# A hybrid SSM and attention layer with experts: scan outputs and turns of k later, queries by block, one norm of o in the output projection

## The chip, the core and the metric

One NeuronCore of a Trainium2 chip runs the whole layer in one launch. The metric is device time in microseconds (us), from one execution of the program. The core's engines run side by side: PE (TensorE, matmuls and transposes), DVE (VectorE) and ACT (ScalarE) and POOL (GpSimd) for element-wise work, SP for issuing DMAs. They meet through semaphores; each engine executes its own instructions in the order in which the program gives them.

## What is computed

One layer, one sequence of 1024 tokens, width 1024, fp32:

```python
mod = silu(c) @ ada_w + ada_b            # sh1, sc1, g1, sh2, sc2, g2
h = rms_norm(x, norm1_g) * (1 + sc1) + sh1
u, q, k, v, f, hc, bg, cg = split(h @ w_in)
y_ssm  = s5(u)              # 16 groups of 16 channels, 64 complex states: scan, gelu, gated unit
y_attn = fox_attention(q, k, v, f)   # 8 heads of 64, causal, q and k normed,
                                     # logits + cum(log f)_q - cum(log f)_k
y_conv = bg * conv3(cg * hc)
y = rms_norm(concat(y_ssm, y_attn, y_conv), per head of 64) * out_norm_g
x = x + g1 * (y @ w_out)
h = rms_norm(x, norm2_g) * (1 + sc2) + sh2
x = x + g2 * moe(h)         # 16 experts in 4 groups, best group, top 2, SwiGLU of width 512
```

## The kernel before, in words

Every fp32 product is made of three matmuls on parts: an operand is split into a high part (ACT, a copy to the matmul's type) and a low part (DVE, the rest); high by high, low by high and high by low are added in PSUM (L293, L295, L298). So each operand costs ACT one pass, DVE one pass and PE three.

The stages, with their time in the profiled execution: modulation and norm of x (to about 55 us); the convolution's projections (to 120); the u projection with the preparation of the scan (`s5_prep`, to 153); q projection, 16 tiles, with the scan (`s5_main`, to 245); k projection, 16 tiles, with the rest of the modulation (`ada2`, to 341); attention (to 534); the w_out stage, 8 tiles of 128 tokens (to 650); routing (to 690); the experts (to the end).

The order is written by hand. Side work is written as generators: `step` advances the scan's by a given number of yields after each projection tile, so the number of plain yields in a generator says beside which tile a piece of it stands. Four such numbers matter here.

- In `s5_prep` two plain yields stand ahead of the four groups pg (L716 and L718 on PE, copied to gk by ACT at L720). Beside them on PE, `conv_norm` puts small matmuls pn (L950) between the matmuls of a u tile; they read zt, which ACT squares at L942 in four pieces.
- `PY` plain yields stand in `s5_main` between the scan's last elementwise steps (vv on DVE) and the four groups py (L855, L856, L858: 4 times 3 matmuls each), which ACT takes through the gelu (L860). Then come eight turns pt (L876, L877) and the gated unit.
- A q or k tile's result (pm, two PSUM buffers) is copied to r by ACT (L1162) with its squares (L1167). After four tiles `qk_norm` puts four steps into a list by the number of tiles by which each is later: norm, split (ks, buffered once), and two turns (L1090 on PE, evicted by ACT or DVE at L1098). `QC, QD` are these distances for q, `KC, KD_` for k.
- In attention, a unit is one head and two blocks of 128 queries with all keys up to them: score (L1298, L1299 with the low part, L1300 the mask), shift by the decay with the running minimum (DVE, L1316), exponential (ACT, L1327), transposes of the logits (L1340), their split into ph (ACT, L1345) and pl (DVE, L95), the product with v (L1360, L1361), and the gather of o (L1374). There are 32 units, four lots m of eight heads; two heads' groups hg of 4 share one load of q, whose parts are kept in DRAM (`qtd`). `load_q` brings both blocks of a group into one tile of 2048 columns; the ring holds one such tile in the first half of the stage and two after head unit 12, where pools are exchanged. At its end the weight rows of w_out are split too (woh on ACT, wol on POOL).

The output norm of attention's o is made per lot of two token blocks by `norm_o(m)`: squares and sums (on POOL for m below `NP`, otherwise ACT and DVE), then an inverse square root in small DVE steps of 128x16 (L1407, L1408, L110 to L115), then the multiplication into o_all. Lots 0, 1 and 2 are made inside attention, lot 3 in the w_out stage, at tiles i = 2 to 4.

The w_out stage, per tile of 128 tokens: `w_prep` transposes the scan's rows (ysm) and o and splits them to yh and yl; `w_mm` makes two halves of 512 columns in PSUM (pmw, two buffers); `w_x1` applies gate and residue on DVE, which frees pmw; `w_h2` makes the second norm, with POOL adding a row and storing. `steps` advances the norm of o between them.

Expert weights are loaded by SP as their buffers come free.

Of the kernel before, what the change touches and what calls it, by code (L numbers as in the profile page):

```python
# [8 lines left out]
F32 = mybir.dt.float32  # L9
# [35 lines left out]
EB = 1  # L45
NP = 3
WS = 48
WT = 4
PB = 4
QC, QD, KC, KD_ = 3, 6, 2, 4  # L50
EA = (1, 0, 0, 2)
# [4 lines left out]
XB = 1  # L56
PY = 5
UG = 6
# [23 lines left out]
def _emit(tc, nc, V, A, G, T, I, out, dump, upto, stack):  # L82
# [11 lines left out]
    def tt(o, a, b, op, eng=None):  # L94
        (eng or V).tensor_tensor(o, a, b, op=op)  # L95
# [547 lines left out]
    def s5_prep():  # L643
# [53 lines left out]
        for n in range(2):  # L697
# [6 lines left out]
            yield  # L704
        yield
        yield

# [511 lines left out]
    with ExitStack() as esa:  # L1219
        pa1 = esa.enter_context(tc.tile_pool(name="pa1", bufs=2, side="right"))  # L1220
        lgr, phr, plr_, qtr = Ring("lg", S), Ring("ph", 512), Ring("pl", 512), Ring("qt", 2048)
        lgr.add(pa1, 3)
        phr.add(pa1, 2)
        plr_.add(pa1, 2)
        qtr.add(pa1, 1)
        ost = pa1.tile([P, 16, HD], F32, name="ost", bufs=1)
# [30 lines left out]

        def load_q(g):

            qt = qtr.tile(F32R)[:].rearrange("p (b n c) -> p b n c", b=2, n=2)  # L1260
            m, hg = g // 2, g % 2
            for b in range(2):
                src = qtd[2 * m + b, hg]
                nc.sync.dma_start(out=qt[:, b, 0, :].bitcast(F32), in_=src)
                nc.sync.dma_start(out=qt[0:64, b, 1, :].bitcast(F32), in_=src[64:P, :])
                nc.sync.dma_start(out=qt[64:P, b, 1, :].bitcast(F32), in_=src[0:64, :])
            qts[m, hg] = qt

# [15 lines left out]
        def score(u, b):  # L1284

            if u >= len(units):
                return
            m, h = units[u]
            w = P * (2 * m + b + 1)
            if (u, b) == (16, 0):  # L1290
                es_s.close()
                ps_s.append(es_s.enter_context(tc.tile_pool(name="ps_s2", bufs=2, space=PSUM)))
            sp = ps_s[-1].tile([P, 512 if m < 2 else S], F32, name="sp", tag="s")
            qt = qts[m, h // 4]
            qs = [qt[:, b, n, (h % 4) * P:(h % 4) * P + P] for n in range(2)]
            for n0 in range(0, w, 512):
                n1 = min(n0 + 512, w)
                T.matmul(sp[:, n0:n1], lhsT=qs[0], rhs=kT[:, h, n0:n1], start=True, stop=False)  # L1298
                T.matmul(sp[:, n0:n1], lhsT=qs[1], rhs=kT[:, h, n0:n1], start=False, stop=n1 != w)  # L1299
            T.matmul(sp[:, w - P:w], lhsT=identB, rhs=maskB, start=False, stop=True)  # L1300
            sps[u, b] = sp
# [83 lines left out]
        def norm_o(m, pool, sq):  # L1385
# [26 lines left out]
            rs = got[0]  # L1412
            tt(ov, ov, rs[:, :, None].to_broadcast([P, 16, HD]), ALU.mult, G if m < 3 else V)

# [20 lines left out]
        def v_end():  # L1435
            while v_done:
                v_out(*v_done.pop(0))

        load_q(0)
        for u in range(2):  # L1440
# [23 lines left out]
        for n, (u, kp) in enumerate(steps):  # L1464
# [14 lines left out]
            for b in bs:  # L1479
                shift(u + 2, b)  # L1480
            v_end()
            if 1 in bs:
                if not second and 4 * len(qts) == u + 3:
                    load_q(len(qts))
                if u == 12:
                    es_v.close()
                    es_w.close()
                    es_h.close()
                    op_ = es_o.enter_context(tc.tile_pool(name="op_", bufs=1, side="left"))
                    o_all = op_.tile([P, NT, NH, HD], F32, name="o_all")  # L1490
                    wo = es_wo.enter_context(tc.tile_pool(name="wo", bufs=1, side="left"))
                    pa = esa.enter_context(tc.tile_pool(name="pa", bufs=2, side="left"))
                    lgr.add(pa, 3)
                    phr.add(pa, PB - 2)
                    plr_.add(pa, PB - 2)
                    qtr.add(pa, 1)
                    for g in saved:
                        nc.gpsimd.dma_start(out=o_all[:, g // 2 * 2:g // 2 * 2 + 2, g % 2 * 4:g % 2 * 4 + 4, :],
                                            in_=od[g].rearrange("p (b h d) -> p b h d", b=2, h=4))
                    norms.append(norm_o(0, pa, ost))  # L1500
                    second = True
                if second and 4 * len(qts) <= u + 4 < len(units):
                    load_q(len(qts))
                load_n(u + 4)
# [8 lines left out]
            if second and len(wait) >= (LW if n > 18 else 1):  # L1513
                finish()
            if h == 1 and kp == m and m > 1:
                norms.append(norm_o(m - 1, pa, ost))
# [216 lines left out]
    with ExitStack() as esw:  # L1733
# [16 lines left out]
        def w_prep(i, ld):  # L1750
# [5 lines left out]
            of = o_all[:, i].rearrange("p h d -> p (h d)")  # L1756
            for k0, n in ((0, 2), (2, 4)):
                pt = ps_y.tile([P, 512], F32, name="pty", tag="y")
# [96 lines left out]
        for i in range(NT):  # L1855
            x1 = x1s[i] = pw.tile([P, D], F32, name="x1", tag="x1")
            pm = w_mm(y, 0)
            if i == 1:
# [4 lines left out]
                V.tensor_copy(c0, pl)  # L1863
            if i == 2:
                last_o = norm_o(3, pw, pw.tile([P, 16, HD], F32, name="sqo", tag="sq", bufs=1))
            if 2 <= i < 5:
                steps(last_o, 2)
            ny = w_prep(i + 1, ld.get(i + 1))
# [431 lines left out]
```

## Time and profile before

| | |
|---|---|
| median of 3 runs (lowest, highest) | 1094.33 us (1094.05, 1100.98) |
| the profiled execution | 1096.41 us, span 1094.7 us |
| PE busy | 1010.8 us, 92% of the span |
| DVE, ACT, POOL busy | 735.6, 520.8, 244.2 us |
| PE's mean granted clock, share of full speed | 0.957 |

The profile is one execution on the hardware. A slice is a fortieth of the span, 27.4 us; busy shares of an engine come in tenths. PEclk is the clock granted to PE, as a share of full speed. In the timeline a row is an instruction or several alike in a row: start, length, engine, line of the kernel, operation, out<-in, shape and, in brackets, the idle time of the engine just before it with what ended it.

### The profile page before, as it was taken

The numbers are of one execution on the slowest core, as the hardware profiler recorded it, in microseconds if no ns is written. First come the engines' busy times: TensorE is split into PE (matmuls) and PEld (weight loads), VectorE is DVE, ScalarE is ACT, GpSimd is POOL, SyncE is SP. The second block draws the span as 40 slices with busy tenths as digits, with TensorE's granted clock in tenths as the row PEclk, the third lists the DMA queues.
The fourth block names the chain that finished last, engine by engine and source line by source line (L and its number), as shares of the span: only waits on it lengthen the run. The fifth ranks groups of instructions, "written<-read, shape, count | busy, mean of one in ns | idle before, by whom it ended". The sixth has DMA issues, their size and how long they took to land. (4 is left out here: it accounts for less than half of the span.)

```text
span 1094.7 us, 17976 instructions
## 1 busy us (share of the span) xinstructions
PE 1010.8 (92%) x6273; PEld 823.8 (75%) x6273; DVE 735.6 (67%) x1608; ACT 520.8 (48%) x1102; POOL 244.2 (22%) x275
## 2 busy tenths in 40 slices
PE   4999999799999998998899994999999999999995
PEld 2767779788778977987788883777777777777774
DVE  5779525826544344787566778896556999789593
ACT  3531214235444555776522223655344676567470
POOL 2019001001110002237222134212333312122121
PEclk9999899879999998998899995999999999999998
DMA  9801145106784444554436625896778899969782
GB/s 316 265 14 46 30 103 104 49 20 228 262 296 147 115 127 120 168 182 147 138 121 212 226 106 188 288 353 230 237 229 285 264 375 358 375 233 356 257 268 42
DMA packets 105472, 215.61 MB, mean 197 GB/s; under 512 B 16658, under 2 KB 39680, under 8 KB 105216
## 3 DMA queue, kind: packets, MB, share of 16 engines
q1 hardware_dynamic: 92368, 171.19, 46.6%
q0 software_dynamic: 12000, 40.37, 13.3%
q10 hardware_dynamic: 992, 2.63, 0.6%
q8 instruction: 61, 1.00, 0.4%
q14 instruction: 51, 0.42, 0.1%
HBM read 185.47 MB, written 28.10 MB: 195 GB/s over the span
## 5 line engine op out<-in xcount | busy, mean ns | idle before, releaser
L95 DVE TENSOR_TENSOR wel<-wer,weh 128x1024 fp32r<-128x1024 f32 x192 | 223.2, 1217 | 2.2 <-DVEq L2170 1.3
L1953 ACT ACTIVATE weh<-wer 128x1024 fp32r<-128x1024 f32 x192 | 189.0, 1053 | 5.1 <-DVE oh L1962 1.7
L2008 POOL DMA_INDIRECT out_dram<-y,idx x28 | 64.2, 2293 | 221.1 <-DVE y L2073 136.3
L2036 PE MATMUL pg<-weh,xh 128*128 128x512 f32 x256 | 104.8, 409 | 2.0 <-ACT hid L2194 0.7
L2037 PE MATMUL pg<-weh,xl 128*128 128x512 f32 x256 | 103.1, 403 | 0.0
L95 DVE TENSOR_TENSOR pl<-ptp,ph 128x512 fp32r<-128x512 f32 (+1 forms) x80 | 50.2, 635 | 38.9 <-ACT ph L1345 38.7
L2041 PE MATMUL pg<-wel,xh 128*128 128x512 f32 x256 | 66.3, 397 | 0.0
L2036 PEld LDWEIGHTS pg<-weh,xh 128*128 128x128 f32 x256 | 49.1, 192 | 17.9 <-issue 6.1
L1345 ACT ACTIVATE ph<-ptp 128x512 fp32r<-128x512 f32 (+1 forms) x80 | 44.1, 553 | 29.7 <-PE ptp L1340 29.4
L2037 PEld LDWEIGHTS pg<-weh,xl 128*128 128x128 f32 x256 | 49.2, 192 | 11.5 <-DVE xl L95 0.4
L2041 PEld LDWEIGHTS pg<-wel,xh 128*128 128x128 f32 x256 | 47.7, 188 | 11.2
L1327 ACT ACTIVATE lg<-lg,mn 128x128 f32<-128x128 f32 (+3 forms) x64 | 49.5, 773 | 11.0 <-DVE mn L1316 11.0
L2063 PE MATMUL pd<-weh,hh 128*128 128x512 f32 x128 | 52.3, 409 | 0.7 <-ACT hh L2055 0.5
L1340 PE MATMUL ptp<-identF,lg 128*128 128x128 f32 x288 | 47.7, 283 | 5.5 <-DVE pl L95 5.3
L293 PE MATMUL pmw<-woh,yh 128*128 128x512 f32 x128 | 52.7, 412 | 0.0
L295 PE MATMUL pmw<-woh,yl 128*128 128x512 f32 x128 | 51.1, 400 | 0.0
L2064 PE MATMUL pd<-wel,hh 128*128 128x512 f32 x128 | 50.6, 395 | 0.0
L2022 ACT ACTIVATE xh<-ptx 128x512 fp32r<-128x512 f32 x32 | 19.2, 599 | 61.8 <-issue 58.6
L1360 PE MATMUL po<-ph,vs 128*128 128x256 f32 (+1 forms) x160 | 47.1, 315 | 1.1 <-ACT ot L1364 1.0
L1162 ACT ACTIVATE r<-pm 128x256 f32<-128x256 f32 x32 | 12.4, 386 | 73.3 <-PE pm L298 54.6
L1992 POOL DMA_INDIRECT xg<-h2d,idx x16 | 22.1, 1380 | 89.2 <-DVE wgt L1979 85.8
L1361 PE MATMUL po<-pl,vs 128*128 128x256 f32 (+1 forms) x160 | 40.2, 285 | 0.1
(660 smaller groups left out, 2635.1 us busy)
## 6 DMA issues: line engine op xcount, KB each, us to landing
wer<-in_w_up_dram SPq DMA_DIRECT2D x64, 512.0 KB
wer<-in_w_gate_dram SPq DMA_DIRECT2D x63, 512.0 KB
wer<-in_w_down_dram SPq DMA_DIRECT2D x63, 512.0 KB
adw<-in_ada_w_dram SPq DMA_DIRECT2D x32, 512.0 KB
vroom<-in_ada_w_dram SPq DMA_DIRECT2D x16, 512.0 KB
xt<-in_x_dram SPq DMA_DIRECT2D x14, 512.0 KB
qtd<-qe POOLq DMA_DIRECT2D x16, 256.0 KB, 7.8
qt<-qtd SPq DMA_DIRECT2D x16, 256.0 KB
```

The lines of the kernel that those rows point to most:

```text
L95: (eng or V).tensor_tensor(o, a, b, op=op)
L293: T.matmul(o, lhsT=sh(k), rhs=mh(k), start=(k == 0), stop=False)
L295: T.matmul(o, lhsT=sl(k), rhs=mh(k), start=False, stop=False)
L1327: A.activation(lg[:, :w], lg[:, :w], AF.Exp, bias=mn, scale=-1.0, accum_out=l_all[:, qb, h:h + 1])
L1340: T.transpose(pt[:, c0:c0 + P], lgs[u, b][0][:, k0:k0 + P], identF)
L1953: A.activation(hi, raw, AF.Copy)
L2008: G.indirect_dma_start(out=out[:, :], out_offset=bass.IndirectOffsetOnAxis(ap=ix, axis=0), in_=y, in_offset=None, compute_op=ALU.add)
L2036: T.matmul(pg, lhsT=x[0][:, k, :], rhs=hi, start=(k == 0), stop=False)
L2037: T.matmul(pg, lhsT=x[1][:, k, :], rhs=hi, start=False, stop=False)
L2041: T.matmul(pg, lhsT=x[0][:, k, :], rhs=lo, start=False, stop=(k == KD - 1))
L2063: T.matmul(pd, lhsT=h[0][:, k, :], rhs=hi[:, n, :], start=(k == 0), stop=False)
L2064: T.matmul(pd, lhsT=h[0][:, k, :], rhs=lo[:, n, :], start=False, stop=False)
```

## The change

Seven numbers or places: four plain yields instead of two in `s5_prep`; `PY` 8 instead of 5; `KD_` 5 instead of 4; `load_q` loads one block of queries into a tile of 1024 columns, in a ring of twice as many tiles; `NP` 2 instead of 3, with which lot 2 of `norm_o` goes to the w_out stage, three steps at tiles 0 and 1 each; and in the first `w_prep` the transposes of o stand ahead of those of ysm.

```diff
-NP = 3
+NP = 2
-QC, QD, KC, KD_ = 3, 6, 2, 4
+QC, QD, KC, KD_ = 3, 6, 2, 5
-PY = 5
+PY = 8
...
-        yield
-        yield
+        for _ in range(4):
+            yield
...
-qtr.add(pa1, 1)
+qtr.add(pa1, 2)
...
-        def load_q(g):
-
-            qt = qtr.tile(F32R)[:].rearrange("p (b n c) -> p b n c", b=2, n=2)
-            m, hg = g // 2, g % 2
-            for b in range(2):
-                src = qtd[2 * m + b, hg]
-                nc.sync.dma_start(out=qt[:, b, 0, :].bitcast(F32), in_=src)
-                nc.sync.dma_start(out=qt[0:64, b, 1, :].bitcast(F32), in_=src[64:P, :])
-                nc.sync.dma_start(out=qt[64:P, b, 1, :].bitcast(F32), in_=src[0:64, :])
-            qts[m, hg] = qt
+        q_at = [0, 0]
+
+        def load_q(b):
+
+            qt = qtr.tile(F32R)[:].rearrange("p (n c) -> p n c", n=2)
+            m, hg = q_at[b] // 2, q_at[b] % 2
+            q_at[b] += 1
+            src = qtd[2 * m + b, hg]
+            nc.sync.dma_start(out=qt[:, 0, :].bitcast(F32), in_=src)
+            nc.sync.dma_start(out=qt[0:64, 1, :].bitcast(F32), in_=src[64:P, :])
+            nc.sync.dma_start(out=qt[64:P, 1, :].bitcast(F32), in_=src[0:64, :])
+            qts[m, hg, b] = qt
...
-            tt(ov, ov, rs[:, :, None].to_broadcast([P, 16, HD]), ALU.mult, G if m < 3 else V)
+            tt(ov, ov, rs[:, :, None].to_broadcast([P, 16, HD]), ALU.mult, G if m < 2 else V)
...
+            for b in bs:
+                if not second and 4 * q_at[b] == u + 3:
+                    load_q(b)
...
-                if second and 4 * len(qts) <= u + 4 < len(units):
-                    load_q(len(qts))
+                for b in range(2):
+                    if second and 4 * q_at[b] <= u + 4 < len(units):
+                        load_q(b)
...
-            if h == 1 and kp == m and m > 1:
+            if h == 1 and kp == m == 2:
...
-            for k0, n in ((0, 2), (2, 4)):
+            for k0, n in ((0, 2), (2, 4)) if i else ((2, 4), (0, 2)):
...
-            if i == 2:
-                last_o = norm_o(3, pw, pw.tile([P, 16, HD], F32, name="sqo", tag="sq", bufs=1))
-            if 2 <= i < 5:
-                steps(last_o, 2)
+            if i in (0, 2):
+                last_o = norm_o(2 + i // 2, pw, pw.tile([P, 16, HD], F32, name="sqo", tag="sq", bufs=1))
+            if i < 5:
+                steps(last_o, 3 if i < 2 else 2)
```

How it moves the instructions, at three places. In the first, ACT in the q projection, r is the copy of a projection tile's result, sq its squares, and the row with py is the gelu of one or two py groups. Before:

```order
L1098 ACTIVATE qe<-ptk 128x512
L1076 ACTIVATE ks<-r_1618 128x16x64
L1162 ACTIVATE r_2063<-pm 128x256
L1167 ACTIVATE sq,ss<-pm 128x64 x4
L280 ACTIVATE wh__1907<-wr__1767 128x2x256
L860 ACT_TABLE_LOAD
L860 ACTIVATE vroom<-py 128x4x8x16 x2
L1162 ACTIVATE r_2063<-pm 128x256
L1167 ACTIVATE sq,ss<-pm 128x64 x4
L860 ACTIVATE vroom<-py 128x4x8x16 x2
```

And of the change:

```order
L1162 ACTIVATE r_2063<-pm 128x256
L1167 ACTIVATE sq,ss<-pm 128x64 x4
L280 ACTIVATE wh__1907<-wr__1767 128x2x256
L1162 ACTIVATE r_2063<-pm 128x256
L1167 ACTIVATE sq,ss<-pm 128x64 x4
L860 ACT_TABLE_LOAD
L860 ACTIVATE vroom<-py 128x4x8x16
L1162 ACTIVATE r_2063<-pm 128x256
L1167 ACTIVATE sq,ss<-pm 128x64 x4
L1098 ACTIVATE qe<-ptk 128x512
L280 ACTIVATE wh__1907<-wr__1911 128x2x256
L860 ACTIVATE vroom<-py 128x4x8x16 x2
```

The first py group now follows two projection tiles instead of one and comes alone; the second and third stand a tile further on, and the fourth behind one more. PE has the same order of tiles and groups.

In the second place, DVE late in attention, pl is the low part of transposed logits, lg and mn the shift, and l, ro_i, ro_y and ro_t are the small steps of the norm of lot 2. Before:

```order
L95 TENSOR_TENSOR pl<-ptp,ph 128x512
L95 TENSOR_TENSOR pl<-ptp,ph 128x384
L1407 SCALAR_TENSOR_TENSOR l_5611<-f_sb 128x16
L1408 SCALAR_TENSOR_TENSOR l_5611<-sso,l_5611 128x16
L95 TENSOR_TENSOR pl<-ptp,ph 128x512
L1316 ISA lg,mn<-sp,nqb 128x896
L1316 ISA mn 128x1
L110 TENSOR_SCALAR ro_i<-l_5611 128x16
L111 TENSOR_SCALAR ro_y<-ro_i 128x16
L113 SCALAR_TENSOR_TENSOR ro_t<-ro_y 128x16
L114 TENSOR_TENSOR ro_t<-ro_t,l_5611 128x16
L115 SCALAR_TENSOR_TENSOR ro_y<-ro_t,ro_y 128x16
```

And of the change, where the line of the shift has become L1318:

```order
L95 TENSOR_TENSOR pl<-ptp,ph 128x512
L95 TENSOR_TENSOR pl<-ptp,ph 128x384
L95 TENSOR_TENSOR pl<-ptp,ph 128x512
L1318 ISA lg,mn<-sp,nqb 128x896
L1318 ISA mn 128x1
```

The small steps are gone from here, and the splits stand as before.

In the third place, DVE at the first tile of the w_out stage, s2r, bs and wrs are rows and weights of the second norm and the router, yl the low part of the next tile, and x the product that frees pmw. Before:

```order
L1836 SCALAR_TENSOR_TENSOR s2r<-s2r,n2r 128x1024
L1842 SCALAR_TENSOR_TENSOR bs_6045<-bs_6045,pv 128x8
L95 TENSOR_TENSOR wrs<-wr,bs_6045 128x128
L95 TENSOR_TENSOR yl<-pty,yh 128x256
L95 TENSOR_TENSOR yl<-pty,yh 128x512
L95 TENSOR_TENSOR yl<-cvt,yh 128x256
L95 TENSOR_TENSOR x_6071<-pmw,g1r 128x512
```

And of the change:

```order
L95 TENSOR_TENSOR wrs<-wr,bs_6027 128x128
L1406 TENSOR_REDUCE sso<-sqo 128x16
L1409 SCALAR_TENSOR_TENSOR l_6083<-f_sb 128x16
L1410 SCALAR_TENSOR_TENSOR l_6083<-sso,l_6083 128x16
L110 TENSOR_SCALAR ro_i<-l_6083 128x16
L111 TENSOR_SCALAR ro_y<-ro_i 128x16
L113 SCALAR_TENSOR_TENSOR ro_t<-ro_y 128x16
L114 TENSOR_TENSOR ro_t<-ro_t,l_6083 128x16
L115 SCALAR_TENSOR_TENSOR ro_y<-ro_t,ro_y 128x16
L95 TENSOR_TENSOR yl<-pty,yh 128x256
L95 TENSOR_TENSOR yl<-pty,yh 128x512
L95 TENSOR_TENSOR yl<-cvt,yh 128x256
```

A reduce and seven small steps now stand between wrs and the first yl; x follows behind the yl as before.

## Rows read from the trace of the kernel before

**Rows 1.** Page, part 2: busy tenths of PE and DMA in 40 slices
```profile
PE   4999999799999998998899994999999999999995
...
DMA  9801145106784444554436625896778899969782
```

**Rows 2.** Windows: stretch, us, busy PE, PEld, DVE, ACT, POOL (instructions); PEclk, DMA share, GB/s
```profile
120.77:152.69 31.92, 29.71 (x145) 22.55 (x144) 7.38 (x21) 6.69 (x12) 0.00 (x0) 0.79 0.23 47
...
206.28:226.55 20.27, 14.77 (x51) 11.03 (x49) 14.29 (x25) 3.60 (x12) 1.63 (x3) 0.62 0.20 65
226.55:231.70 5.15, 5.15 (x25) 5.15 (x25) 0.00 (x0) 0.60 (x1) 0.00 (x0) 0.51 0.00 0
231.70:240.12 8.42, 8.42 (x51) 6.48 (x49) 0.00 (x0) 1.80 (x10) 0.00 (x0) 1.00 0.01 2
```

**Rows 3.** Timeline of PE and ACT, u projection (start, us, instruction, idle before)
```profile
122.54 0.39 PE L718 MATMUL pg<-can,vroom 64*16 64x128 f32 x2 [1.38 <-DVE can L693]
...
125.49 0.38 PE L950 MATMUL pn<-blkF,zt 128*128 128x2 f32 x2 [0.81 <-ACT zt L942]
...
121.37 0.64 ACT L280 ACTIVATE wh__1211<-wr__1011 128x528 fp32r<-128x528 f32 x1
...
124.82 2.17 ACT L942 ACTIVATE zt<-hcs 128x512 f32<-128x512 f32 x4
```

**Rows 4.** Timeline of PE and ACT, first py groups
```profile
209.00 0.49 PE L856 MATMUL py<-car,vv 64*128 64x128 f32 x2 [2.34 <-DVE vv L95]
212.65 0.79 PE L858 MATMUL py<-can,vv 64*128 64x128 f32 x2 [3.16 <-DVE vv L95]
...
218.76 0.39 ACT L1162 ACTIVATE r<-pm 128x256 f32<-128x256 f32 x1 [13.21 <-DVE rk_m L123]
```

**Rows 5.** Timeline of PE, k projection
```profile
297.21 0.54 PE L1090 MATMUL ptk<-identR,ks 128*128 128x128 f32 x4 [2.12 <-ACT qe L1098]
```

**Rows 6.** Waits: engine, line, waited for: us in total, times, longest
```profile
PE sp L1299 <- DMA qt<-qtd: 4.5, 5, 1.9
```

**Rows 7.** Timeline of PE, POOL and DVE, late in attention
```profile
495.65 0.55 PE L1374 MATMUL oT<-ii,ot 128*128 128x64 f32 x4
502.11 0.56 PE L1374 MATMUL oT<-ii,ot 128*128 128x64 f32 x4
510.29 0.55 PE L1340 MATMUL ptp<-identF,lg 128*128 128x128 f32 x3 [2.87 <-DVE pl L95]
511.15 0.63 PE L1374 MATMUL oT<-ii,ot 128*128 128x64 f32 x4
521.22 0.56 PE L1374 MATMUL oT<-ii,ot 128*128 128x64 f32 x4
...
506.84 2.34 POOL L95 TENSOR_TENSOR wol<-wor,woh 128x1024 fp32r<-128x1024 f32 x1
...
506.94 2.28 DVE L113 SCALAR_TENSOR_TENSOR ro_t<-ro_y 128x16 f32<-128x16 f32 x1
509.46 0.17 DVE L115 SCALAR_TENSOR_TENSOR ro_y<-ro_t,ro_y 128x16 f32<-128x16 f32 x1
```

**Rows 8.** Windows: the low clock in attention's last units (columns as in rows 2)
```profile
511.75:518.45 6.70, 5.94 (x22) 4.85 (x21) 4.05 (x10) 4.88 (x8) 4.28 (x2) 0.51 0.04 13
```

**Rows 9.** Timeline of PE and DVE, w_out stage
```profile
536.53 0.66 PE L1761 MATMUL pty<-identF,ysm 128*128 128x128 f32 x2 [2.64 <-DMA cvt<-cd]
552.07 0.39 PE L293 MATMUL pmw<-woh,yh 128*128 128x512 f32 x1
...
550.33 0.68 DVE L95 TENSOR_TENSOR x<-pmw,g1r 128x512 f32<-128x512 f32 x1
565.58 0.69 DVE L95 TENSOR_TENSOR x<-pmw,g1r 128x512 f32<-128x512 f32 x1 [2.50 <-PE pmw L298]
571.44 1.21 DVE L1404 TENSOR_REDUCE sso<-sqo 128x16 f32<-128x1024 f32 x1
585.91 2.35 DVE L111 TENSOR_SCALAR ro_y<-ro_i 128x16 int32<-128x16 int32 x1
```

More of the change, by code (lines that the diff above doesn't have):

```diff
@@ L1220, in _emit @@
         pa1 = esa.enter_context(tc.tile_pool(name="pa1", bufs=2, side="right"))
-        lgr, phr, plr_, qtr = Ring("lg", S), Ring("ph", 512), Ring("pl", 512), Ring("qt", 2048)
+        lgr, phr, plr_, qtr = Ring("lg", S), Ring("ph", 512), Ring("pl", 512), Ring("qt", 1024)
         lgr.add(pa1, 3)
@@ L1293, in score @@
             sp = ps_s[-1].tile([P, 512 if m < 2 else S], F32, name="sp", tag="s")
-            qt = qts[m, h // 4]
-            qs = [qt[:, b, n, (h % 4) * P:(h % 4) * P + P] for n in range(2)]
+            qt = qts[m, h // 4, b]
+            qs = [qt[:, n, (h % 4) * P:(h % 4) * P + P] for n in range(2)]
             for n0 in range(0, w, 512):
@@ L1437, in v_end @@
                 v_out(*v_done.pop(0))
-        load_q(0)
+        for b in range(2):
+            load_q(b)
         for u in range(2):
@@ L1481, in _emit @@
             v_end()
+            for b in bs:
+                if not second and 4 * q_at[b] == u + 3:
+                    load_q(b)
             if 1 in bs:
-                if not second and 4 * len(qts) == u + 3:
-                    load_q(len(qts))
                 if u == 12:
@@ L1495, in _emit @@
                     plr_.add(pa, PB - 2)
-                    qtr.add(pa, 1)
+                    qtr.add(pa, 2)
                     for g in saved:
@@ L1501, in _emit @@
                     second = True
-                if second and 4 * len(qts) <= u + 4 < len(units):
-                    load_q(len(qts))
+                for b in range(2):
+                    if second and 4 * q_at[b] <= u + 4 < len(units):
+                        load_q(b)
                 load_n(u + 4)
```

## The prediction

> **What bounds the kernel now.** I read the page's slices first: TensorE (PE) is nearly full in all but the first slices, and in the long second half, the experts, it stands at 8 and 9 while the DMA engines stand at 7 to 9, not full throughout [rows 1]. So a microsecond that PE saves ahead of the experts should come out at the end, as long as the expert weights, loaded as buffers come free, move forward with it. The question is then where PE waits and where its granted clock is low ahead of the experts. The waits of PE by what ended them, and the timeline around each, lead to five places that the diff touches: the u projection, the first py groups in the q projection, the turns of k, the last head units of attention, and the first tiles of the w_out stage. Windows over these give the clock. In the rows the reader is to look at the bracket (idle before, and who ended it) and at PEclk: 1.00 is 2.4 GHz, about 0.5 is 1.2 GHz.
>
> **The change part by part.** The profiled execution took 1096.41 us (span 1094.7, the rest lies around it); the median of the runs shown is 1094.33. All terms below are differences, and I apply the sum to the median.
>
> *1. pg two steps later.* PE waits 1.38 us at the first pg group for can, which VectorE (DVE) has just begun, and 0.81 us at the first pn for the square zt on ScalarE (ACT) [rows 3]. The second wait is made by the first: gk, which needs pg, stands ahead of the four squares on ACT, so they start at 124.82 though ACT's split ended at 122.01 [rows 3]. After, the squares follow that split directly; the first is done some 0.6 us later (2.17 for four), and pn, which PE now reaches right after 120.77 and one matmul, waits about 1.6 us in one piece. Idle: 2.19 less 1.6, -0.6. The u projection's 31.92 us ran at a mean clock of 0.79 with PE busy 29.71 [rows 2]: with a lower level of half the speed, 0.21 of this is 6.7 us at stake. The idle piece comes earlier, but it is not smaller than each of the two before, so I expect most of the low clock again and count a fifth of the 6.7 back: -1.4. **-2.0** (from -5, the clock mostly held, to +1, the second pg group that now stands later among the pn pairs costing a third low piece).
>
> *2. py three steps later.* Before, PE reaches py at 206.28, two tiles ahead of its data, waits 2.34 us for the first half of vv and 3.16 for the second, and both py groups then run mostly at the lower level: 20.27 us for 24 matmuls with PEclk 0.62, against 8.42 for the next two py groups at 1.00 [rows 2, 4]. The project tile behind them still runs at 0.51, in 5.15 us [rows 2]; half of that, 2.6, at full speed. Lost before: 20.27 - 8.42 + 2.55 = 14.4 us, of which 5.5 are idle. After (the order rows), one more project tile stands ahead of py0 and fills 206.3 to about 209.1. The data of vv are made by DVE, whose chain the change does not touch, so its second half still comes at 212.65 [rows 4] and py0 waits about 2.7 of it. Then a new wait: the tile after py0 needs a PSUM buffer of pm, of which there are two, and both are held by tiles that ACT empties only from 218.76 on, when DVE's q norm lets it [rows 4]. With py0 done at 216.0 to 216.5, PE idles about 3 us more. Idle after: 5.7, no less than before. What is gained is the low stretch: py1 is no longer behind the gap, so one py group and one tile (3.2 + 2.6, the first being half of 14.77 - 8.42) can be low instead of two groups and a tile; I take 4.4 for it, some of this having come back by then. 14.4 - 5.7 - 4.4 = **-4.3** (from -8.7, no low clock at all, to 0, as long a low stretch as before).
>
> *3. Turns of k one tile later.* The ptk transposes wait once for ACT's qe buffer, 2.12 us [rows 5]; a project tile later ACT has had about 3 us more. The tile that comes ahead needs nothing from them. **-1.5** (-2.1, the wait, to +1, the last turns falling into the v tiles).
>
> *4. q by block.* Scores wait five times for the load of qt, 4.5 us in all, longest 1.9 [rows 6]. The ring holds the same bytes before and after; what a block gains is that its half comes free after its own score, one unit step sooner, and that the first score does not wait for the second half's three transfers. The two longest waits stand where the pools are changed at head unit 12 and the ring is refilled; there the transfers come in the same order as before. So only the other waits shrink: **-1.0** (-3 to 0).
>
> *5. Norm 2 out of attention's tail.* Here the trace is plainest. One head unit, from its gather of o to the next, takes 6.46 us (495.65 to 502.11); the next two take 9.04 and 10.07 [rows 7], 6.2 us more. In them small DVE steps of the norm, 0.17 each elsewhere, stand between the splits pl for which PE waits: L113 takes 2.28 beside GpSimd's (POOL's) wol of 2.34, and PE waits 2.87 us [rows 7]. Behind it the clock falls, 0.51 over 6.70 us with PE busy 5.94 [rows 8]. The SBUF page of the Trainium skill ("SBUF — State Buffer", the section on SBUF's two sides) says the port pair that VectorE and GpSimd share is locked for a whole instruction and the other engine fully blocks; 2.28 beside 2.34, against 0.17, agrees with that here. After, those nine DVE steps are gone and the POOL adds with them; wol stays, but the splits pl read PSUM and ran beside it before. Both units should come near 6.46 (6.2 less, of which I take 6): **-6.0** (-6.3; or -2.9, its one wait, if only the wait goes and ACT, busy 4.88 of the 6.70 [rows 8], becomes the pace).
>
> *6. First w_out tile turns o first.* PE waits 2.64 us there for the last load of the scan's rows [rows 9]. The matmuls behind need all of yh, so the four transposes of o fill the wait but the start stays: **-0.5** (-2 to 0).
>
> *7. Norm 2 in w_out.* At i = 0 DVE gets a reduce of 1.21 [rows 9] and seven small steps of about 0.2, some 2.6 us, ahead of yl and of the product x that frees PSUM. x starts at 550.33 and takes 0.68, the next tile wants the buffer at 552.07 [rows 9]: 1.06 us of room, so PE waits 1.5; yl a little more. The Square on ACT follows the row s2r and has room. At i = 1 six small steps and a multiply (1.2) come. They may meet POOL's add of h: then one takes 2.35 (L111 [rows 9]). Even so DVE waits 2.50 for PE at the second x of this tile [rows 9], and the first x frees a buffer wanted a whole tile later; nothing there. **+1.9** (0, slack that I don't see, to +5, the wait with a low clock behind it).
>
> Sum: -2.0 - 4.3 - 1.5 - 1.0 - 6.0 - 0.5 + 1.9 = -13.4. 1094.3 - 13.4 = **1081 us**.
>
> **The rivals.**
> (a) *The early waits only move.* Idle stays about the same in terms 1 and 2 by my own count (2.19 to 1.6, 5.5 to 5.7), so if the low stretches return in full, both terms are near 0: 1094.3 - 7.1 = 1087. For it: the gap at pm is new and 3 us. Against: the group py1 runs away from the gap. Chance 0.16.
> (b) *The clock holds at both.* Terms 1 and 2 become -5 and -8.7: 1094.3 - 13.4 - 3.0 - 4.4 = 1074. For it: the gaps are cut into pieces with matmuls between. Against: pieces of 1.38 and 0.81 were enough before [rows 2, 3]. Chance 0.16.
> (c) *Slower: py at the lower level throughout.* py1 to py3 and the tiles among them now alternate after two gaps. If all run low, each py costs 3.2 and each of three to five tiles 2.6 more: 17 to 23 us against the 4.4 I counted. Then 1081 + 13 to 1081 + 19, 1094 to 1100, and with 3 or 4 us more from terms 1 and 7, up to 1104 to 1106. It decides once low pieces there cost over 18 us, that is all three groups and four tiles. Against: one tile at the lower level was enough to bring the clock back before, and the next two groups ran at 1.00 [rows 2]. Chance 0.08.
> (d) *Norm 2 only moves its cost.* Tail -2.9 instead of -6.0, and w_out +5 instead of +1.9: 1081 + 6.2 = 1087. For it: at i = 0 the steps stand on the path again. Against: no wol runs there. Chance 0.11.
>
> **How the numbers follow.** My forecast (terms as summed, own range 1075 to 1087) gets 0.49. About 1% is what a measurement of this kernel can tell from no change: below 1083.4 is faster. Of the 0.49, 0.37 lies below it and 0.12 above; (b) is all faster, (a) and (d) lie within 1%, of (c) half exceeds 1105. Faster 0.37 + 0.16 = 0.53; same 0.12 + 0.16 + 0.11 + 0.04 = 0.43; slower 0.04. The range goes from 1072, below the centre of (b), to 1092, above (a) and (d), and leaves out (c) and half of (b), 0.16.
>
> **What would show it.** In the changed profile: no PE wait above 1 us for pl in the last attention units and a head unit of about 6.5 us there (term 5, on which the most hangs); one wait for pm or for ACT's r near 216 to 219, py1 and py2 together in about 8.4 us (term 2); u projection shorter than 31.9 (term 1); PE waiting 1 to 2 us for pmw's buffer at the second w_out tile (term 7). What would make it wrong above all: the clock, whose low stretches hold 5.7 of the 13.4 here (1.4 and 4.3) and can take as much again, and expert weights that arrive no earlier than before, so that PE waits for them at the first expert.

## The result

The change is faster: the ratio of its time to that of the kernel before, from 16 runs of each, is 0.9895, with a 95% interval from 0.9873 to 0.9917; the medians are 1086.53 and 1099.36 us. That is 11.5 us saved (9 to 14), against the 13.4 of the sum. The predicted 1081 stood on the median of three early runs of before, 1094.33; with the measured ratio these would give 1082.8. The profiled execution of the change has a span of 1087.7 us, 7.0 shorter than that of before; why one pair of profiles shows less than the medians do is told under the table of stages.

The page of the change, part 2, busy tenths in 40 slices:

```profile
PE   3999999999999998999899994999999999999995
...
PEclk9999879989999999999999995999999999999998
DMA  9801236137783443563446626896778899979782
```

As in [rows 1], PE is full nearly everywhere and the DMA engines are not throughout, in the experts too. The eighth slice of PE, in which the first py group begins, was a 7 before and is a 9 now.

Windows of the change over the stretches of [rows 2] (stretch, us, busy PE, PEld, DVE, ACT, POOL with their instructions, then PEclk, DMA share, GB/s):

```profile
122.48:157.41 34.93, 32.70 (x145) 24.65 (x143) 7.46 (x21) 6.68 (x12) 0.00 (x0) 0.71 0.15 37
214.04:224.58 10.54, 7.21 (x26) 5.25 (x24) 7.61 (x14) 1.25 (x10) 1.63 (x3) 0.66 0.30 100
224.58:229.54 4.96, 4.96 (x33) 4.96 (x33) 3.93 (x8) 3.88 (x15) 0.00 (x0) 0.68 0.00 0
229.54:237.95 8.41, 8.41 (x50) 6.48 (x49) 1.39 (x2) 2.37 (x11) 1.07 (x2) 1.00 0.60 174
```

The first row is the u projection, 3.0 us longer than before in this profile, at a lower clock. The second is py0 alone, the third the project tile behind it with eight turns of q, the fourth py1 and py2 at full clock.

Timeline of PE, change, the waits that answer to [rows 3, 4] (idle before in brackets):

```profile
124.38 0.38 PE L950 MATMUL pn<-blkF,zt 128*128 128x2 f32 x2 [1.50 <-ACT zt L942]
139.66 0.39 PE L716 MATMUL pg<-car,vroom 64*16 64x128 f32 x2 [0.68 <-ACT gk L720]
...
217.58 0.79 PE L858 MATMUL py<-can,vv 64*128 64x128 f32 x2 [2.74 <-DVE vv L95]
...
224.58 0.58 PE L293 MATMUL pm<-wh__1503,hTh 128*128 128x256 f32 x1 [0.60 <-ACT sq L1167]
```

In the u projection a second wait, of 0.68 for gk at the later pg groups, has come in beside the one for zt. Of the two waits for vv, 2.34 and 3.16, one of 2.74 is left, and the new wait for pm is there with 0.60.

Timeline of PE and DVE, change, late in attention and in the w_out stage, answering to [rows 7, 9]:

```profile
498.08 0.56 PE L1376 MATMUL oT<-ii,ot 128*128 128x64 f32 x4
504.51 0.55 PE L1376 MATMUL oT<-ii,ot 128*128 128x64 f32 x4
510.54 0.55 PE L1342 MATMUL ptp<-identF,lg 128*128 128x128 f32 x3 [0.76 <-DVE pl L95]
511.40 0.56 PE L1376 MATMUL oT<-ii,ot 128*128 128x64 f32 x4
527.14 0.41 PE L1766 MATMUL pty<-identF,ysm 128*128 128x128 f32 x2 [1.19 <-DMA cvt<-cd]
544.31 0.47 PE L293 MATMUL pmw<-woh,yh 128*128 128x512 f32 x1 [2.75 <-DVE x L95]
...
539.34 0.17 DVE L1847 SCALAR_TENSOR_TENSOR bs<-bs,pv 128x8 f32<-128x8 f32 x1 [1.26 <-DMA bs<-modd]
543.48 0.68 DVE L95 TENSOR_TENSOR x<-pmw,g1r 128x512 f32<-128x512 f32 x1
```

The two head units that took 9.04 and 10.07 take 6.43 and 6.89; the wait for pl of 2.87 is 0.76. At the second w_out tile PE waits 2.75 us for x, where it did not wait before.

Since the traces repeat each stage closely, the stages are set side by side in one table, in us. The stretches run from the first matmul of one kind to the first of the next: u projection to px (the scan's first matmul); px to the first tile of k; from there to the first score; to the last gather of o; from the first to the last matmul of w_out (pmw); and the experts, from their first matmul to the start of PE's last row.

| kernel | u to px | px to k | k to scores | attention | w_out | experts |
|---|---|---|---|---|---|---|
| before | 66.1 | 70.3 | 103.9 | 178.7 | 111.6 | 404.2 |
| the change | 69.3 | 60.9 | 105.2 | 172.6 | 115.3 | 403.3 |
| the change, again (a_same) | 66.4 | 61.9 | 108.2 | 172.9 | 116.5 | 402.3 |
| p_prep: four yields alone | 62.9 | 70.5 | 105.5 | 177.2 | 111.6 | 403.4 |
| p_py: PY 8 alone | 74.5 | 61.5 | 107.7 | 177.2 | 111.5 | 403.3 |
| p_py10: PY 10 alone | 66.0 | 65.2 | 104.7 | 176.8 | 111.6 | 404.0 |
| p_rest: turns of k, q by block, o first | 74.3 | 69.9 | 102.3 | 177.8 | 111.1 | 403.5 |
| p_norm: norm 2 moved, alone | 66.4 | 70.0 | 104.3 | 175.0 | 113.4 | 404.2 |
| p_nowol: before, no subtraction on POOL | 67.1 | 70.3 | 105.2 | 172.3 | 111.4 | 407.5 |
| p_gap: before, norm 2's steps two later | 66.4 | 70.1 | 104.0 | 174.6 | 111.5 | 402.9 |
| a_noprep: change, two yields again | 67.0 | 61.9 | 107.8 | 173.9 | 115.7 | 402.6 |
| a_late: change, norm 2 a tile later | 63.4 | 61.9 | 106.1 | 171.9 | 119.7 | 403.0 |
| a_gap8: change, norm 2 in attention, six later | 63.1 | 62.0 | 105.2 | 173.5 | 111.9 | 403.1 |
| a_gap8_bs: the same, bs loaded earlier | 63.0 | 62.0 | 105.5 | 173.5 | 116.6 | 404.1 |

Between the experts' first matmul and the end nothing is lost of what was saved ahead of them: 404.2 before, 402 to 404 with the change's parts. The change's profile is only 7.0 us shorter than that of before for two reasons that lie ahead of px: its u projection is the 3.2 us longer of the first column, in which kernels of the same order differ by 8 us, and its first matmul of u comes at 115.97 instead of 114.18, behind code that the change leaves as it was.

### The profile page after: what moved, and what is told of

It is laid out like the page before. It is cut to its first block, busy times and chain, and to the rows that moved or that the text cites. A ratio compares the mean times of both kernels' runs of the same rounds, so it can differ in the third digit from the quotient of the medians.

```text
span 1087.7 us, 17979 instructions
## 1 busy us (share of the span) xinstructions
PE 1007.8 (93%) x6273; PEld 820.1 (75%) x6273; DVE 735.6 (68%) x1610; ACT 521.0 (48%) x1103; POOL 232.6 (21%) x267
## 3 DMA queue, kind: packets, MB, share of 16 engines
q0 software_dynamic: 12000, 40.37, 13.4%
## 5 line engine op out<-in xcount | busy, mean ns | idle before, releaser
L2041 PE MATMUL pg<-weh,xh 128*128 128x512 f32 x256 | 104.3, 407 | 2.0 <-ACT hid L2199 0.7
L1329 ACT ACTIVATE lg<-lg,mn 128x128 f32<-128x128 f32 (+3 forms) x64 | 49.5, 774 | 11.1 <-DVE mn L1318 10.9
```

Of the source, the lines that this page charges most:

```text
L1329: A.activation(lg[:, :w], lg[:, :w], AF.Exp, bias=mn, scale=-1.0, accum_out=l_all[:, qb, h:h + 1])
L2041: T.matmul(pg, lhsT=x[0][:, k, :], rhs=hi, start=(k == 0), stop=False)
```

## The experiments

**One part alone, four kernels.** Each is the kernel before with one part of the change. The edits are the lines of the diff; p_rest takes three parts together.

```diff
 p_py
-PY = 5
+PY = 8
 p_prep
-        yield
-        yield
+        for _ in range(4):
+            yield
 p_norm
-NP = 3
+NP = 2
...
+                last_o = norm_o(2 + i // 2, pw, pw.tile([P, 16, HD], F32, name="sqo", tag="sq", bufs=1))
 p_rest
-QC, QD, KC, KD_ = 3, 6, 2, 4
+QC, QD, KC, KD_ = 3, 6, 2, 5
...
+        def load_q(b):
...
+            for k0, n in ((0, 2), (2, 4)) if i else ((2, 4), (0, 2)):
```

> The kernel before with PY 8 alone. Theory: of the change's gain, the py groups carry the most; the two profiles show tile ends moving by 9.0 us between the first px and the end of the q projection (from +4.9 to -4.05), as PE waits 3.3 us there instead of 5.5 and fewer matmuls run at 1.2 GHz. Then 7 to 9 us faster than before, ratio 0.992 to 0.994, with one wait of about 2.7 us for vv in the trace and two of the py groups at PEclk 1.00. Rival: the clock at py differs from run to run whatever the order, and the gain alone is 0 to 3 us.

> The kernel before with lot 2 of the output norm moved to the w_out stage alone. Theory: the two profiles show attention's last units 5.7 us shorter, and 3.7 us given back in the w_out stage, where PE waits 2.75 us at the second tile for the product x and the clock drops once; net 1 to 3 us faster, ratio 0.997 to 0.999. Rival: the loss in w_out is chance of the clock in one profile and the net gain is 5 to 6 us, ratio 0.995.

> The kernel before with four yields ahead of the pg groups alone. In the one profile of the change the u projection took 34.9 us against 31.9, with more of it at 1.2 GHz. Theory: this is the order's doing, and the part alone makes the kernel 1 to 3 us slower, ratio 1.001 to 1.003. Rival, the prediction: 2 us faster, ratio 0.998, and the profile's loss was chance of the clock.

> The kernel before with the turns of k one tile later, the queries by block and the first w_out tile's order alone. Theory: nearly nothing, -3 to 0 us (predicted -1.5, -1.0 and -0.5); in the trace the wait of 2.12 us for qe in the k projection is gone and the waits for qt are down from 4.5 us to 2 or 3. Rival: what the profile of the change shows as a wait of 2.57 us for the modulation's weights in the k projection comes with it, and the part is worth +1 to 0 us.

| part alone | ratio to before (95% interval) | us | predicted |
|---|---|---|---|
| p_py | 0.9939 (0.9911 to 0.9968) | -6.7 | -4.3 |
| p_norm | 0.9981 (0.9949 to 1.0013) | -2.1 | -4.1 |
| p_prep | 1.0005 (0.9972 to 1.0038) | +0.5 | -2.0 |
| p_rest | 0.9977 (0.9950 to 1.0004) | -2.5 | -3.0 |

The us are the ratio less 1, times 1097.4, the median of before in that group. They add up to -10.8, close to the whole change's -11.5, but that sum is known to some 6 or 7 us only, so it does not show that the parts don't meet. Only p_py's interval leaves out 1; the others are read from the traces.

The py groups carry the most, as that theory has it. The stretch from px to k is 69.9 to 70.5 us in all six kernels with PY 5 and 60.9 to 62.0 in all seven with PY 8. The timeline of PE in p_py shows the same two waits as the change:

```profile
221.50 0.49 PE L858 MATMUL py<-can,vv 64*128 64x128 f32 x2 [2.72 <-DVE vv L95]
...
228.85 0.58 PE L293 MATMUL pm<-wh__1503,hTh 128*128 128x256 f32 x1 [1.53 <-ACT sq L1167]
```

Some of the 9 us is given back: the gated unit and some turns of the scan now fall into the k projection, and PE's waits for the modulation's weights are longer there (2.4 to 3.9 us in all in the kernels with PY 5, 3.0 to 5.8 in those with PY 8), so k to scores takes 105 to 108 instead of 104 to 105.5 (p_rest, which moves the turns of k, left aside). From px to the first score p_py takes 169.2 us and before 174.2.

For p_prep the time says no difference; windows from u's first matmul to px (columns as above) of before, p_prep and p_py:

```profile
114.18:180.31 66.13, 63.91 (x409) 53.33 (x409) 23.12 (x48) 18.48 (x73) 4.49 (x8) 0.90 0.44 90
```

```profile
115.03:177.92 62.89, 60.44 (x409) 51.30 (x409) 23.14 (x48) 18.46 (x73) 4.49 (x8) 0.95 0.46 94
```

```profile
114.68:189.15 74.47, 71.74 (x409) 58.05 (x409) 23.13 (x48) 18.44 (x73) 4.49 (x8) 0.79 0.39 79
```

The first and the third are the same instructions in the same order, 409 matmuls with the same DVE, ACT and POOL time, and still 8.3 us apart: PEclk is 0.90 and 0.79. Of eight profiles with two yields, six took 66 to 67 us and two 74; of six with four yields, four took 63, one 66 and one 69. The profiled runs of the two with 74, 1097.33 and 1100.87 us, lie 6 us above the medians of their kernels, which speaks for the run and not the kernel as its cause. So the order is worth 3 us where the clock is kind to both, and the clock is worth more and comes and goes between runs. Where the 3 us come from, the first 20 us of the stage show, in before and in p_prep:

```profile
114.18:134.18 20.00, 17.80 (x78) 14.29 (x79) 10.21 (x11) 5.51 (x11) 0.00 (x0) 0.79 0.16 40
```

```profile
115.03:135.03 20.00, 18.27 (x104) 14.21 (x104) 10.93 (x12) 6.80 (x14) 0.00 (x0) 1.00 0.20 54
```

Behind the one wait of 1.50 the clock stays at 1.00, in five of the six profiles with four yields; in the change's own it is 0.83. The idle time is the same, 1.50 and 0.68 in place of 1.38 and 0.81. The traces speak against the theory that the order loses here and for the gain that was predicted; the times, with 3.6 us either way, leave both open.

p_rest's trace has no wait for qe left at the turns of k, and k to scores is 102.3, the shortest of all: 1.6 less than before. The rival's wait of 2.57 us for the modulation's weights is not there; the longest is 1.3. The waits for qt did not shrink: 5.1 us in all, after 4.5.

**Is the limit at py the data alone?** The kernel before with PY 10, one more projection tile ahead of py0.

```diff
-PY = 5
+PY = 10
```

> The kernel before with PY 10: py0 yet one projection tile later than in the change. Theory: what is left of the idle time at py with PY 8 (2.7 us for vv, 0.6 to 1.5 for ACT) can't be had by waiting longer, since the third tile needs a PSUM buffer that ACT frees only when DVE's chain is done: PE then stands for pm, some 8 to 10 us in one piece, ahead of that tile and vv is there long before; slower than PY 8 by 2 to 6 us, ratio to before 0.996 to 1.000. Rival: the data of vv is the only limit, the wait for it vanishes, and PY 10 is 3 us faster than PY 8, ratio 0.991.

Ratio 0.9989 (0.9955 to 1.0023), 5.5 us behind p_py. The timeline of PE:

```profile
220.15 0.58 PE L293 MATMUL pm<-wh__1503,hTh 128*128 128x256 f32 x1 [10.14 <-ACT sq L1167]
```

The waits for vv are gone and one of 10.14 us stands in their place, ahead of the third tile: both pm buffers wait for ACT, and ACT waits for DVE's q norm. DVE's chain is not DVE's work alone; ahead of the norm it stands for a store that empties its qe buffer (timeline of DVE):

```profile
216.97 0.69 DVE L1096 COPY qe<-ptk 128x512 f32<-128x512 f32 x1 [2.46 <-DMA qtd<-qe]
```

In before this wait is 3.05 us and in the change 2.69. So DVE's chain, with that store in it, sets the stretch, and PY 8 is the place in which PE has two tiles and one py group to fill it with; what the chain would gain from an earlier store no run here shows. The stages bear out less than the times: px to k is 3.7 us longer than in p_py, but k to scores 3.0 shorter, and the two intervals overlap.

**Why was the norm slow in attention?** Two kernels, with one run of each. In p_nowol POOL only zeroes the low parts of the first four rows of w_out, so the low part's products are left out; norm 2's steps stay. In p_gap the steps come two steps of the loop later.

```diff
 p_nowol
-                tt(lo, wraw[k], hi[:].bitcast(F32), ALU.subtract, G)
+                G.memset(lo[:].bitcast(F32), 0.0)
 p_gap
                 tt(ss, sq[:, :, 0], sq[:, :, 1], ALU.add, G)
-                yield
-                yield
+                for _ in range(4 if m == 2 else 2):
+                    yield
```

> The kernel before, in which POOL only zeroes the low parts of the first four w_out rows late in attention instead of making them by a subtraction (so the low part's products are left out of the result). Norm 2's small DVE steps stay where they were. Theory: the small steps are short by themselves (0.17 us each) and become 2.28 only beside POOL's subtraction of 2.34; without it L113 takes 0.2, PE's wait of 2.87 us for pl falls under 1, and the two slow head units (19.1 us together) take 13 to 15. Rival: the steps' number and place on DVE makes the wait, whatever POOL does; it stays over 2 us.

> The kernel before with norm 2's small DVE steps two steps of attention's loop later, nothing else moved: they then stand between two of POOL's subtractions rather than in one. Theory: most of the wait of 2.87 us goes though the norm stays in attention, and the two slow head units take 14 to 16 us instead of 19.1. Rival: the steps cost the same anywhere in this stretch, 18 to 19 us.

Timeline of DVE and POOL, p_nowol, the step that took 2.28 us before:

```profile
508.82 0.17 DVE L113 SCALAR_TENSOR_TENSOR ro_t<-ro_y 128x16 f32<-128x16 f32 x1
...
507.58 0.97 POOL L1248 MEMSET wol<- 128x1024 f32 x1
```

And p_gap:

```profile
507.54 1.36 DVE L1407 SCALAR_TENSOR_TENSOR l<-f_sb 128x16 f32<-128x16 f32 x1
...
513.19 1.45 DVE L113 SCALAR_TENSOR_TENSOR ro_t<-ro_y 128x16 f32<-128x16 f32 x1
...
506.50 2.36 POOL L95 TENSOR_TENSOR wol<-wor,woh 128x1024 fp32r<-128x1024 f32 x1
...
512.21 2.40 POOL L95 TENSOR_TENSOR wol<-wor,woh 128x1024 fp32r<-128x1024 f32 x1 [3.34 <-ACT woh L1247]
```

Without POOL's subtraction the same step takes 0.17, PE's largest wait for pl in this stretch is 0.65, and the two slow head units take 13.7 us instead of 19.1 (gathers at 504.68 and 518.34), though all of the norm's steps are there. In p_gap two steps still begin inside a subtraction and end with it (507.54 + 1.36 = 508.90, and 506.50 + 2.36 = 508.86); the units take 15.1 (501.46 to 516.58). So it is the meeting, not the number of steps. That agrees with the Trainium skill, "SBUF — State Buffer", its section on SBUF's two sides, by which, of a VectorE instruction with two SBUF inputs and a GpSimd one that reads SBUF, the later is blocked until the other ends. Moving norm 2 out gives 13.3 (the change, and p_norm with gathers at 503.84 and 517.15). The 19.1 of before is the upper end: p_prep, p_py, p_py10 and p_rest, which have the norm where before has it, take 18.9, 17.6, 17.5 and 17.9. And the unit behind the two takes 5.5 us where the norm is out, instead of 4.9 to 5.0.

**What does the w_out stage lose?** The change with norm 2 begun a tile later there, and with norm 2 back in attention, behind POOL's last subtraction; the second also with an earlier load.

```diff
 a_late
-            if i in (0, 2):
+            if i in (1, 3):
...
-            if i < 5:
-                steps(last_o, 3 if i < 2 else 2)
+            if 1 <= i < 6:
+                steps(last_o, 3 if i < 3 else 2)
 a_gap8
-NP = 2
+NP = 3
...
-                yield
-                yield
+                for _ in range(8 if m == 2 else 2):
+                    yield
 a_gap8_bs (beside that)
-        ld = {0: w_loads(0), 1: w_loads(1)}
+        ld = {0: w_loads(0)}
+        bs2 = pw.tile([P, 2, KD], F32, name="bs2", bufs=1)
+        nc.sync.dma_start(out=bs2, in_=ap_of(modd, D, [[1, P], [D, 2], [P, KD]]))
+        ld[1] = w_loads(1)
```

> The changed kernel with norm 2 begun one tile later in the w_out stage (three steps at tiles 1 and 2 each, norm 3 at tiles 3 to 5), so that at tile 0 nothing stands ahead of the product x. Theory: the loss in w_out (PE's wait of 2.75 us for x there, 1.54 in the kernel with this part alone, and the clock behind it) is made by the place at tile 0, where x has 1.06 us of room; a tile later DVE has room, the wait is gone, and the kernel is 2 to 4 us faster than the change: 12 to 15 us faster than before, ratio 0.986 to 0.989. Rival: any place in w_out costs DVE's order the same, the wait reappears at tile 1 or 2, and the time is that of the change, ratio 0.9895.

> The changed kernel with norm 2 back in attention, its small DVE steps six steps of the loop later than before the change, behind the last of POOL's subtractions there. Theory: it keeps attention's tail as short as the change has it (two slow head units in 13 to 14 us) and gives back what the change lost in the w_out stage (PE's wait for x at the second tile, 1.5 to 2.75 us, and what the clock adds): 2 to 4 us faster than the change. Rival: what the w_out stage loses comes from its own loads, which come late whenever attention ends earlier (1.6 us of wait were left with norm 2 a tile later); then this kernel is within 1 us of the change and PE still waits over 1 us at the second tile.

> The same, with the load of the router's row sums bs issued before the second tile's loads instead of behind all loads of the stage. Theory: DVE stands for this load ahead of x (1.3 to 2.4 us in all profiles); issued earlier, the wait is gone, x comes 1 us or more earlier and no wait is left at the second tile even where the loads run late: 0 to 2 us faster than without it. Rival: the load lands no earlier, because it is its many small pieces that take the time and not its place; no difference.

In p_norm the wait at the second tile is what the prediction worked out, 1.5 us, and no low stretch follows it. Its time, -2.1 with 3.5 either way, fits that theory's 1 to 3 us and just reaches the rival's 5 to 6; w_out, 1.8 us longer than in before, speaks against the rival.

```profile
550.07 0.47 PE L293 MATMUL pmw<-woh,yh 128*128 128x512 f32 x1 [1.54 <-DVE x L95]
```

a_late is no better than the change but, at 0.9945 (0.9919 to 0.9972), probably worse. Its timeline of PE says why:

```profile
537.68 0.47 PE L293 MATMUL pmw<-woh,yh 128*128 128x512 f32 x1 [1.60 <-DVE x L95]
604.13 0.63 PE L1766 MATMUL pty<-identF,o_all 128*128 128x128 f32 x4 [3.50 <-DVE o_all L95]
```

The second wait comes with the edit itself: norm 3, pushed to tiles 3 to 5, comes too late for the transposes of the next tile. The first is the rival's: with no step of norm 2 ahead of x it is still 1.60, since DVE stood 2.37 us for the load of bs. a_gap8 has the norm back in attention and nearly all of the loss is gone, w_out 111.9 instead of 115.3 and 116.5, with this left:

```profile
537.18 0.47 PE L293 MATMUL pmw<-woh,yh 128*128 128x512 f32 x1 [0.72 <-DVE x L95]
```

In attention it is as short late on (13.3 us for the two units, 0.4 more in the next). Stage by stage it is 2.5 to 4 us better than the change; the times can't tell them apart: 0.9888 (0.9837 to 0.9939), and the change run beside it 0.9897 (0.9849 to 0.9946).

> The changed kernel itself, run beside the others of this group as their measure. Ratio to before 0.987 to 0.992.

a_gap8_bs shows what the load was worth. DVE no longer waits for bs, which it reads at 532.24 in place of 534.68, and no wait for x is left; but the second tile's own loads stand behind it now (timeline of PE):

```profile
532.87 0.69 PE L1766 MATMUL pty<-identF,ysm 128*128 128x128 f32 x2 [1.68 <-DMA ysm<-yd]
```

A low stretch of the clock goes with it (the 8 us from 528 on have a PEclk of 0.79), and w_out takes 116.6. The second tile begins 17.95 us after the first instead of 14.51, which is most of this; the later tiles take 14.5 us each instead of 14.3, for which the runs show no reason. Both sides of that expectation fell: the load lands earlier, and the stage is slower. The time is 0.9897 (0.9859 to 0.9935).

**Four yields inside the change.** The change with two yields again.

```diff
-        for _ in range(4):
-            yield
+        yield
+        yield
```

> The changed kernel with two yields again ahead of the pg groups. The part alone gave 1.0005. Theory: the u projection's time is set by which stretches run at 1.2 GHz, and this differs between runs of one order (10 to 14 us low in four profiles, 31 us in two, with two yields; 7 and 20 us with four); the order has no steady worth, and this kernel lies within 2 us of the change. Rival: four yields save about 3 us when all else is the change's, and this kernel is 3 us slower than the change.

0.9915 (0.9879 to 0.9950) beside the change's 0.9897: 2 us, well inside the intervals, on the side of the four yields. Its u to px is 67.0, as with two yields elsewhere.

## Why the prediction was right, point by point

The sum (-13.4) and the size (11.5 saved, 9 to 14) agree, and the time lies in the range. That they come so near is in part luck, since terms were mis-sized in opposite directions: term 2 gave 2.4 more than predicted, terms 5 and 7 together 2 (p_norm's time) to 5 (the change's stages) less.

1. *pg later, predicted -2.0.* The first step held: the squares follow the split directly and pn waits once, 1.50 for the 1.6 worked out. Uncounted was the wait of 0.68 for gk at the later pg groups, with which the idle time is 2.18 instead of 2.19; the -0.6 for it is not there, and the gain is all clock, of which only a fifth was counted. Between the common levels the traces give -3 (63 against 66 to 67 us); the times of the part alone, +0.5 with 3.6 either way, don't confirm it. What I did not see is that the low clock here differs between runs of one order by more than the term's whole range.
2. *py later, predicted -4.3, measured -6.7 alone.* The mechanism held: one tile ahead, one wait for vv of 2.7 (predicted 2.7), a new wait for pm, one group and one tile at the low level instead of two groups and a tile, the next two groups at 1.00 in 8.41. Mis-sized was the wait for pm: 3 us predicted, 0.60 measured (1.53 in p_py). I let py0 end at 216.0 to 216.5; with the lower level over nearly all of it, it ends at 224.0, 219.1 on the scale of before, and ACT frees the buffer 0.6 later. So idle time is 3.3 instead of 5.7, and the low clock costs 4.5 where 4.4 was taken (7.21 for py0 against half of 8.42, and 4.3 against 2.8 for the tile); with these the same sum gives 14.4 - 3.3 - 4.5 = 6.6. Beyond my terms, two waits of 0.69 for qe ahead of turns of the scan (at 244.94 and 250.24 in before) are gone too. The rest of the 9 us in px to k is work that moved into k.
3. *Turns of k, -1.5.* The wait of 2.12 is gone, k to scores 1.6 shorter in p_rest.
4. *q by block, -1.0.* No gain can be seen: the scores' waits for qt are 4.7 to 6.6 us in the profiles with it, 4.5 to 6.8 in those without. The longest (2.5 in the change) stands, as before, where the pools change at head unit 12, a place that the change leaves as it was; that the other waits would shrink was wrong.
5. *Norm 2 out of attention, -6.0.* The two units are 5.8 us shorter than in before and 4.2 to 5.6 shorter than in the four other kernels with the norm in its place; the unit behind them gives 0.6 back. So the term is some 4 to 5, and before's profile, from which it was taken, the worst of the five. The reason given, POOL's subtraction beside the small steps, is shown by p_nowol.
6. *o first, -0.5.* From the last gather to the first pmw 4.56 before, 4.09 with it; over all profiles 4.1 to 4.3 with it and 4.2 to 4.6 without.
7. *Norm 2 in w_out, +1.9.* Alone it is that (111.6 to 113.4, the wait 1.54). In the change it is +3.7 to +4.9 in three profiles (a_noprep is the third), near the upper bound. Failed was the slack of 1.06, taken from the trace of before. x hangs on the load of bs as well, which came 11.3 to 12.6 us after the stage's first matmul in two profiles of the change and 10.9 in that of before; and PE wants the buffer 13.5 us after that matmul in the change, 14.3 in before. So no room is left, and the wait is 2.75 to 3.8. The second tile begins 2.0 us later than in before (16.28 after the first, 14.28 there) and then takes 15.8 us instead of 14.1, at a mean PEclk of 0.89 instead of 1.00; behind the waits of 0.72 to 1.60 in p_norm, a_late and a_gap8 it takes 14.2.

Of the rivals, (a), the waits only move, is out at py: px to k is about 9 us shorter in every profile with PY 8, and px to the first score still 4 to 8; in the u projection only the traces speak against it. (b), a clock that holds, is out: one low stretch stayed at py in each. (c) is out, since py1 to py3 run at 1.00 in the change. (d) was half right: the price in w_out is near its +5, the gain in attention is not its -2.9 but 4 to 5. The chance of a gain over 1% (0.53) met a ratio whose interval lies on both sides of that line.

## What to carry over

Before moving a chain of small DVE steps to another stage, look at what POOL runs beside them: here moving them two to six steps, away from POOL's subtractions, does, by the stages, most of what moving them to another stage did, without its price there. A wait that a later place removes is limited by the next wait behind it (here the PSUM buffer that ACT empties): read that second wait's time first, and what that engine waits for in turn (here DVE, and behind it a store). Of the three places tried, the last one ahead of it was the best by the times. Slack read off one profile is worth no more than the loads that it hangs on repeat between profiles.

## What the runs showed of the hardware

The clock of one and the same stretch of instructions differs between runs: 66.1 and 74.5 us from u's first matmul to px, at a mean PEclk of 0.90 and 0.79, with equal instructions and equal times on the other engines. In the next stage it repeats: from px to k the profiles of equal PY agree within 1.1 us. So one stage can hide or feign a gain of 8 us, and only many runs or a comparison stage by stage tells. What decides between the two levels there stays open; that the u projection puts small matmuls (pn, pg) between large ones may be the reason, but no run here shows it. The length of a wait alone does not tell either: at the second w_out tile the clock fell behind waits of 2.75 to 3.8 us and not behind those of 0.72 to 1.60, while in the u projection of before it fell with waits of 1.38 and 0.81 us only.
